# Nearest-neighbour upsampling by two: stores of whole runs against pairs of stores in rows of 512 bytes

## The chip, the cores and the metric

The kernel runs on one core of a Trainium2 chip. The metric is the device time of one execution in microseconds (us); the profiled execution is a separate one, and its span (first to last instruction) is a little shorter than its own time. The engines that do work here are VectorE (DVE) and ScalarE (ACT), which copy, SyncE (SP), which issues transfers, and the 16 DMA engines, which move bytes between DRAM and the on-chip memory (SBUF, 128 partitions).

## The reference

An image batch of 16 x 64 x 64 x 64 float32 is doubled in height and width by repeating each element:

```python
def reference(x, scale_factor):          # scale_factor is 2
    ...
    for i in range(new_h):
        for j in range(new_w):
            src_i = i // scale_factor
            src_j = j // scale_factor
            result[:, :, i, j] = x[:, :, src_i, src_j].copy()
```

So every input element appears four times: twice along its row, and the doubled row (a line of 128 elements, 512 bytes) twice, one below the other. 16.78 MB are read and 67.11 MB written.

## The kernel before

The input's 65,536 rows of 64 elements are spread over the 128 partitions, R = 512 rows to each (`xp`, line 173). An output row of the view `op` (line 174) holds both output lines of one input row, upper then lower, 256 elements or 1 KB, and a partition's 512 output rows are contiguous in DRAM.

The input is loaded whole into `xt`, in three DMAs cut at rows 32 and 288 (lines 192 to 195). `begin_before_barrier` moves these three loads ahead of the program's opening barrier. The output is made in nine chunks of 38 to 63 rows (`rows`, line 181). For each chunk, in the loop from line 204 on, DVE copies the first part of the rows (line 213) and ACT the rest (line 214). `expanded` (line 197) is a view of `xt` in which an element is read twice along its row and each row twice, so the copy writes all four. Then SP issues one store (line 215), whose share in each partition is one contiguous run, both in SBUF and in DRAM: k rows of 1 KB.

The on-chip space is one tile `mem`: 79 rows' worth of free output space, and the input behind it. Even chunks lie at the start of the tile, odd chunks end at the input's first row that hasn't been copied yet, so that output grows into input that is no longer needed. The framework puts in the waits: a copy waits for the load of its rows and for the stores that still read the space it writes, a store waits for the copies of its chunk. All DMAs are issued from SP and go through one queue. `close_early` rearranges the end of the program, so that all but the last store's semaphore are dealt with while that store is under way.

Of the kernel before, what the change touches and what calls it, by code (L numbers as in the profile page):

```python
# [153 lines left out]
@with_exitstack  # L154
def kernel(
    ctx: ExitStack,
    tc: tile.TileContext,
    x: bass.AP,
    scale_factor: int,
    out: bass.AP,  # L160
):
    nc = tc.nc
    nc.at_finalize(begin_before_barrier)
    nc.at_finalize(close_early)
    P = nc.NUM_PARTITIONS
    s = int(scale_factor)
    B, C, H, W = x.shape
    R = B * C * H // P
    fdt = x.dtype

    xp = x.rearrange("b c h w -> (b c h) w").rearrange("(p r) w -> p r w", p=P)
    op = out.rearrange("b c (h hd) w -> (b c h) (hd w)", hd=s).rearrange(
        "(p r) w -> p r w", p=P
    )

    rows = [54, 38, 54, 61, 54, 63, 63, 63, 62]
    GROW = s * s
    FREE = 79
    WF = FREE * GROW * W
    assert sum(rows) == R
    mem_pool = ctx.enter_context(tc.tile_pool(name="mem", bufs=1))
    mem = mem_pool.tile([P, WF + R * W], fdt, name="mem")
    xt = mem[:, WF:].rearrange("p (r w) -> p r w", r=R)

    HEAD = 32
    cuts = [0, HEAD, R // 2 + HEAD, R]
    for lo, hi in zip(cuts, cuts[1:]):
        nc.sync.dma_start(out=xt[:, lo:hi], in_=xp[:, lo:hi])  # L195

    def expanded(r0, r1):
        return (
            xt[:, r0:r1].unsqueeze(2).unsqueeze(4).to_broadcast([P, r1 - r0, s, W, s])
        )  # L200

    r0 = 0
    before = (0, 0)
    for n, k in enumerate(rows):
        size = k * GROW * W
        at = 0 if n % 2 == 0 else WF + r0 * W - size
        assert at >= before[1] or at + size <= before[0]
        before = (at, at + size)
        u = mem[:, at : at + size].rearrange(
            "p (k a w b) -> p k a w b", k=k, a=s, w=W  # L210
        )
        kv = k - 1 if n == 0 else k * 5 // 8 & ~1
        nc.vector.tensor_copy(out=u[:, :kv], in_=expanded(r0, r0 + kv))  # L213
        nc.scalar.copy(out=u[:, kv:], in_=expanded(r0 + kv, r0 + k))  # L214
        nc.sync.dma_start(out=op[:, r0 : r0 + k, :], in_=u)  # L215
        r0 += k


# [33 lines left out]
```

## Time and profile before

| | before |
|---|---|
| runs shown | 197.31 and 197.48 us, median 197.39 |
| profiled execution | 196.92 us, span 195.6 |
| DVE busy | 52.3 us, 9 copies |
| ACT busy | 42.1 us, 9 copies and a table load |
| DMA | 83.89 MB, mean 429 GB/s |
| loads | 1, 8 and 7 MB (1024, 8192 and 7168 KB), landing 4.7, 23.6 and 40.1 us after issue |
| stores | 9 of 4864 to 8064 KB, landing 18.8 to 32.6 us after issue |

The profile counts an engine as busy while it copies. DMA engines are counted apart, as a share of all 16; a transfer's time from issue to landing includes its waiting behind earlier ones in the same queue. Besides the page, the trace keeps a record of every DMA packet with its start, duration and size.

### The profile page before, as it was taken

The page shows a single profiled execution, that of the slowest core. Times are in us where ns is not written, and L with a number is a line of the kernel's source. Part 1 is how long each engine was busy: PE and PEld are TensorE (multiplying, and loading weights), DVE is VectorE, ACT ScalarE, POOL GpSimd, SP SyncE. Part 2 cuts the span into 40 slices and gives each one's busy share as a digit, 9 for nine tenths or more (in the row PEclk, how much of TensorE's full clock was granted, in tenths as well). Part 3 has the DMA queues.
Part 4 walks back from the last instruction along what each step waited for, and adds up shares of the span by engine and source line. Part 5 has one row for each costly group of instructions (what it writes and reads, how often), then busy time and mean ns, then how long its engine had stood idle before and what let it go on. Part 6 is the DMA issues. An engine that isn't in the chain of part 4 may idle for free.

```text
span 195.6 us, 102 instructions
## 1 busy us (share of the span) xinstructions
DVE 52.3 (27%) x9; ACT 42.1 (21%) x10; POOL 0.2 (0%) x4
## 2 busy tenths in 40 slices
DVE  0000099940026091053008204500540073000000
ACT  2000000160029700059500004970000073000000
POOL 0000000000000000000000000000000000000000
DMA  9999989889899989999999899999999999999994
GB/s 429 429 429 429 402 375 563 375 362 543 362 436 390 555 362 418 486 409 409 409 420 532 362 531 433 422 422 422 422 422 422 422 422 422 422 435 545 467 428 208
DMA packets 1728, 83.89 MB, mean 429 GB/s; under 512 B 192, under 2 KB 192, under 8 KB 192
## 3 DMA queue, kind: packets, MB, share of 16 engines
q1 hardware_dynamic: 1728, 83.89, 99.2%
HBM read 16.78 MB, written 67.11 MB: 429 GB/s over the span
## 4 chain that ended last, share of the span: by engine, by line
DMA 65%; ACT 11%; DVE 7%; SPq 0%; issue 0%; DVEq 0%; ACTq 0%
DMA out_dram<-mem 53%; DMA mem<-in_x_dram 12%; ACT mem L214 11%; DVE mem L213 7%; SPq L195 0%; DVEq L213 0%; ACTq L214 0%; SPq L215 0%
## 5 line engine op out<-in xcount | busy, mean ns | idle before, releaser
L213 DVE COPY mem<-mem 128x9728 f32<-128x9728 f32 (+3 forms) x9 | 52.3, 5818 | 110.9 <-DMA out_dram<-mem 86.8
L214 ACT COPY mem<-mem 128x6400 f32<-128x6400 f32 (+5 forms) x9 | 40.8, 4530 | 119.4 <-DMA out_dram<-mem 84.2
L214 ACT ACT_TABLE_LOAD x1 | 1.3, 1283 | 1.7 <-PEq L233 1.7
L233 POOL MEMSET const-bfloat16-1.0<- 128x1 bf16 x1 | 0.1, 102 | 0.0
L233 POOL MEMSET const-uint8-127<- 128x1 uint8 x1 | 0.1, 102 | 0.0
L233 POOL MEMSET const-float32-1.0<- 128x1 f32 x1 | 0.1, 99 | 0.0
L233 POOL MEMSET const-float32-0.0<- 128x1 f32 x1 | 0.1, 98 | 0.2 <-issue 0.2
## 6 DMA issues: line engine op xcount, KB each, us to landing
out_dram<-mem SPq DMA_DIRECT2D x3, 8064.0 KB, 32.4
out_dram<-mem SPq DMA_DIRECT2D x3, 6912.0 KB, 22.9
out_dram<-mem SPq DMA_DIRECT2D x1, 7936.0 KB, 32.3
out_dram<-mem SPq DMA_DIRECT2D x1, 7808.0 KB, 29.3
mem<-in_x_dram SPq DMA_DIRECT2D x1, 7168.0 KB, 40.1
out_dram<-mem SPq DMA_DIRECT2D x1, 4864.0 KB, 26.7
mem<-in_x_dram SPq DMA_DIRECT2D x1, 1024.0 KB, 4.7
mem<-in_x_dram SPq DMA_DIRECT2D x1, 23.6
```

What stands on the lines that cost most here:

```text
L213: nc.vector.tensor_copy(out=u[:, :kv], in_=expanded(r0, r0 + kv))
L214: nc.scalar.copy(out=u[:, kv:], in_=expanded(r0 + kv, r0 + k))
L233: nc = _bacc.Bacc("TRN2", target_bir_lowering=False, num_devices=1)
```

## The change

The copies now double elements along the row only: the wide row (128 elements) is in SBUF once. There are eight chunks of 64 rows, in two buffers of their own, `wide`, beside the whole input. Each chunk is stored by two DMAs from the same SBUF rows: one writes the upper output lines, one the lower. In SBUF a partition's 64 wide rows are contiguous; in DRAM each line of 512 bytes is followed by the 512 bytes of the other line, which the other DMA writes. The first two chunks are copied by ACT alone, chunk 1 first; the others by DVE (40 rows) and ACT (24 rows). The loads are cut at rows 48 and 304.

```diff
-    rows = [54, 38, 54, 61, 54, 63, 63, 63, 62]
-    GROW = s * s
-    FREE = 79
-    WF = FREE * GROW * W
-    assert sum(rows) == R
+    N = 8
+    k = R // N
+    size = k * s * W
     mem_pool = ctx.enter_context(tc.tile_pool(name="mem", bufs=1))
-    mem = mem_pool.tile([P, WF + R * W], fdt, name="mem")
-    xt = mem[:, WF:].rearrange("p (r w) -> p r w", r=R)
-    HEAD = 32
+    xt = mem_pool.tile([P, R, W], fdt, name="x")
+    wide = [mem_pool.tile([P, k, W, s], fdt, name=f"wide{b}") for b in range(2)]
+
+    HEAD = 48
     cuts = [0, HEAD, R // 2 + HEAD, R]
     for lo, hi in zip(cuts, cuts[1:]):
         nc.sync.dma_start(out=xt[:, lo:hi], in_=xp[:, lo:hi])
 
-    def expanded(r0, r1):
-        return (
-            xt[:, r0:r1].unsqueeze(2).unsqueeze(4).to_broadcast([P, r1 - r0, s, W, s])
-        )
-
-    r0 = 0
...
-        kv = k - 1 if n == 0 else k * 5 // 8 & ~1
-        nc.vector.tensor_copy(out=u[:, :kv], in_=expanded(r0, r0 + kv))
-        nc.scalar.copy(out=u[:, kv:], in_=expanded(r0 + kv, r0 + k))
-        nc.sync.dma_start(out=op[:, r0 : r0 + k, :], in_=u)
-        r0 += k
+    def widen(n, kv):
+        u = wide[n % 2]
+        for engine, lo, hi in ((nc.vector.tensor_copy, 0, kv), (nc.scalar.copy, kv, k)):
+            if lo < hi:
+                source = xt[:, n * k + lo : n * k + hi].unsqueeze(3)
+                engine(
+                    out=u[:, lo:hi], in_=source.to_broadcast([P, hi - lo, W, s])
+                )
+
+    def store(n):
+        u = wide[n % 2].rearrange("p k w b -> p k (w b)")
+        lines = op[:, n * k : (n + 1) * k, :].rearrange("p k (a w) -> p k a w", a=s)
+        for a in range(s):
+            nc.sync.dma_start(out=lines[:, :, a], in_=u)
+
+    widen(1, 0)
+    widen(0, 0)
+    store(0)
+    store(1)
+    for n in range(2, N):
+        widen(n, k * 5 // 8)
+        store(n)
```

More of the change, by code (lines that the diff above doesn't have):

```diff
@@ L195 @@
         nc.sync.dma_start(out=xt[:, lo:hi], in_=xp[:, lo:hi])
-    def expanded(r0, r1):
-        return (
-            xt[:, r0:r1].unsqueeze(2).unsqueeze(4).to_broadcast([P, r1 - r0, s, W, s])
-        )
-    r0 = 0
[L203 to L211, printed above, removed]
-        kv = k - 1 if n == 0 else k * 5 // 8 & ~1
-        nc.vector.tensor_copy(out=u[:, :kv], in_=expanded(r0, r0 + kv))
-        nc.scalar.copy(out=u[:, kv:], in_=expanded(r0 + kv, r0 + k))
-        nc.sync.dma_start(out=op[:, r0 : r0 + k, :], in_=u)
-        r0 += k
+    def widen(n, kv):
[18 more added lines that the diff above has]
+        store(n)
 _INS = ['x', 'scale_factor']
```

## The prediction

> **What bounds the kernel now.** I began with the page's DMA rows, because the kernel has nothing but copies and transfers.
>
> ```profile
> DMA  9999989889899989999999899999999999999994
> ...
> q1 hardware_dynamic: 1728, 83.89, 99.2%
> HBM read 16.78 MB, written 67.11 MB: 429 GB/s over the span
> ```
>
> The first line is the busy share of the 16 DMA engines in 40 slices of the 195.6 us span, the second gives the queue's packets, megabytes and share of the engines' time. 1728 packets are 12 transfers (3 loads, 9 stores) of 128 partition rows, 1536 in all, and 16 small packets behind each transfer that raise its semaphore. 99.2% of 195.6 us is 194.0 us of work on each engine. Its sixteenth of the bytes is 5.243 MB, which makes 27.0 GB/s per engine.
>
> Next the rate by stage:
>
> ```profile
> 85.00:120.00 35.00, 9.71 (x3) 10.51 (x3) 0.00 (x0) 1.00 1.00 432
> 120.00:158.00 38.00, 10.47 (x3) 11.09 (x3) 0.00 (x0) 1.00 1.00 435
> ```
>
> The last two columns are the DMA share and GB/s in two stretches of the stores: the engines are full, at 432 to 435 GB/s. Then the chain of work that ended last:
>
> ```profile
> DMA 65%; ACT 11%; DVE 7%; SPq 0%; issue 0%; DVEq 0%; ACTq 0%
> ...
> 0.42 23.59 DMA mem<-in_x_dram
> ...
> 24.11 14.30 DVE mem L213
> ...
> 38.48 18.82 DMA out_dram<-mem
> ```
>
> Read alone it gives ACT and DVE 18% of the span and invites one to shorten copies. It must be laid beside the DMA rows: the chain follows one transfer at a time, and while a copy on it runs another transfer is moving bytes. In the trace's records of single DMA packets 16 are under way (for some ns at a hand-over 17) from the ramp at 1.0 us to 194.8 us, also at 40 us where the last loads hand over to the first store. So the time is the sum of the packets on each engine. A copy counts only if it leaves the queue empty.
>
> **The price of one packet.** In these records a packet lasts its bytes at 27.2 GB/s plus about 8 ns: 38,912 bytes take 1439 ns (1430.6 + 8.4), 55,296 take 2041 (2032.9 + 8.1), 64,512 take 2380 (2371.8 + 8.2), 65,536 take 2418 (2409.4 + 8.6). The next packet on the same engine starts 3 to 4 ns before the end (found by following starts to ends, so an estimate). The net fixed cost is thus 4.2 to 5.1 ns; I take 4.6. The semaphore packets of 4 bytes last 9 ns and overlap by 3 to 6, which nets 3 to 6 ns: the same cost with no data in it.
>
> **Part 1, stores in rows of 512 bytes.** Before, a partition's share of a store is one run of 38 to 63 KB. After, line a of the 64 rows is 64 runs of 512 bytes with 512 bytes skipped between them in DRAM. Bytes stay 67.11 MB. A store DMA has 128 x 64 = 8192 runs, 512 per engine; 16 DMAs make 8192 per engine, where there were 9 x 8 = 72. No packet of such data is in the trace, so its cost is bounded by the rows above: 512 bytes at 27.2 GB/s are 18.8 ns, and the fixed part lies between nothing (runs of one row flow together) and 9 ns (the whole 4-byte packet, with no overlap). I take 4.6 ns, since the net cost is the same from 38,912 to 65,536 bytes and hardly less at 4 bytes, so 512 lies between rows that agree. One run is then 23.4 ns and the stores are 8192 x 23.42 = 191.9 us, where they now are 154.2 us of data plus 72 x 4.6 ns = 154.5 us. **That is +37.4 us**, wholly on the path since nothing but these packets sets it. The ends are +0.1 us and 8192 x 27.8 = 227.9 us, +73.4 us.
>
> The Trainium skill ("DMA: Bandwidth & Descriptors", section "Why small descriptors are slow (HBM only)") puts the cost inside the DMA engine at about 3 cycles for each packet, whatever its size. At the 850 MHz that the page gives that is 3.5 ns, and the sum would by an estimate come to 226 us; the trace's packets, at a net 4.2 to 5.1 ns, show rather more.
>
> **Part 2, the opening.** The loads are cut at rows 48 and 304 instead of 32 and 288. The first two chunks need rows 0 to 127, so both wait for the second load; its 16 further rows (0.52 MB at 435 GB/s) land 1.2 us later, at 24.0 + 1.2 = 25.2 us. Both chunks are then copied by ACT alone, one behind the other, chunk 1 first, each 64 x 128 = 8192 elements. The rows:
>
> ```profile
> L214 ACT COPY mem<-mem 128x6400 f32<-128x6400 f32 x3 | 16.6, 5525 | 24.4 <-DMA out_dram<-mem 24.3
> L214 ACT COPY mem<-mem 128x5632 f32<-128x5632 f32 x2 | 9.8, 4886 | 33.0 <-DMA out_dram<-mem 33.0
> ...
> L214 ACT COPY mem<-mem 128x256 f32<-128x256 f32 x1 | 0.4, 405 | 21.0 <-DMA mem<-in_x_dram 21.0
> ```
>
> The mean ns stands after the busy time. From 5632 to 6400 elements 639 ns are added, 0.832 ns an element; 256 elements leave 192 ns fixed. 8192 elements take 7.0 us, two of them 14.0, so the first store is issued at about 39.3 us where it was 38.48. Its first byte follows some 1.0 us later (as in the first load), at 40.3. The loads' packets end between 39.6 and 40.5 us, depending on the engine. The hole is 0 to 0.8 us; I take 0.3. DVE's 14.3 us at this place goes, which gains nothing, as it was covered by the third load.
>
> **Part 3, half the copying afterwards.** Chunks 2 to 7 give DVE 40 rows (5120 elements) and ACT 24 rows (3072).
>
> ```profile
> L213 DVE COPY mem<-mem 128x9728 f32<-128x9728 f32 x5 | 26.1, 5227 | 59.7 <-DMA out_dram<-mem 59.7
> ...
> L213 DVE COPY mem<-mem 128x13568 f32<-128x13568 f32 x1 | 14.3, 14285 | 24.1 <-DMA mem<-in_x_dram 24.1
> ```
>
> DVE has two speeds here, 0.537 and 1.053 ns an element, so 5120 take 2.75 or 5.4 us; all calls with an even row count are fast, and 40 is even. ACT takes 192 + 3072 x 0.832 ns = 2.75 us. DVE's sum falls from 52.3 to 6 x 2.75 = 16.5 us. I cost that gain at nothing: those 59.7 us of idle time were spent waiting for a store to land.
>
> A new wait comes with the two buffers: chunk n's copies wait until both DMAs of store n-2 have landed. Behind them on SP stand store n's two issues, and nothing else. Meanwhile store n-1 is queued whole, 8.4 MB, 1024 runs per engine, 24.0 us by my price and 19.3 us with no fixed cost. The copy, up to 5.4 us, and about 1 us from issue to first byte fit in. Were the cover gone, 6 x (2.75 + 1.0) = 22 us would be added.
>
> **Part 4, issuing.** SP issues 16 stores instead of 9.
>
> ```profile
> L215 SPq DMA_DIRECT2D out_dram<-mem x9: 332/332/348, 38.5 to 163.2; - x9
> ```
>
> Seven more at 0.33 us are 2.3 us beside 24 us of transfer each time: nothing. All issues of before carry 128 rows, so the trace doesn't show whether one with 8192 runs takes longer.
>
> **Sum.** The profiled execution took 196.92 us (span 195.6 and 1.3 around it). 196.92 + 37.4 + 0.3 = 234.6 us. The median of the runs shown is 0.47 higher at 197.39, so I predict **235 us**.
>
> **Rivals.**
>
> *The runs of a row flow together (not slower).* If the fixed cost is paid once per row and not per 512-byte run, for instance because the skip is only an address step, the stores stay at 154.5 us and the total is 196.9 + 0.1 + 0.3 + 0.5 = 198 us. For it: 8 ns of a packet overlap in part already, and the source is one contiguous run in SBUF. Against: the 4-byte packet nets as much as one of 64 KB, so the cost goes with the packet, not its bytes. It decides below 0.5 ns a run (+4 us). The Trainium skill on the same page (section "Specifications") gives 512 bytes as the smallest transfer that reaches line rate, and by that rule the change is neutral; no transfer in the trace is small enough to test it. Chance 0.09.
>
> *Nothing overlaps with small runs.* If the next run cannot start before the last one's end, the full 8.2 ns count: 8192 x 27.0 = 221.3 us, +66.8, total 264.5 us. For it: the overlap of 3 to 4 ns was seen only where the engine had microseconds to look ahead. Against: the 4-byte packets overlap too. Chance of this or a smaller loss of overlap, 245 to 272 us: 0.20.
>
> *The descriptors aren't made fast enough.* The generator must make 131,072 runs. If all of the 332 ns of an issue went with its 128 rows, 2.6 ns each, they would take 340 us, and the total would be 40 + 340 + 2 = 382 us. It decides from 191.9 us / 131,072 = 1.46 ns a run on, that is, if more than 187 of the 332 ns go with rows. DRAM pages being written in halves would show in the same place. Against: a load and a store issue of 128 rows each, of very different sizes, take 332 to 432 ns, which looks like a cost per instruction. Chance of over 272 us: 0.09.
>
> **Chances and range.** The forecast, 222 to 245 us, has 0.60; with 0.20, 0.09 and 0.09 for the rivals, 0.02 is left for faster, as the data alone need 192.8 us on each engine and no byte is saved. About 2% is what a measurement of this kernel can tell from no change. Slower: 0.60 + 0.20 + 0.09 = 0.89; same 0.09; faster 0.02. The range begins with the smallest net cost of a 4-byte packet, 3 ns: 8192 x 21.8 = 178.8 us, +24.3, 222 us. It ends with 9 ns and no overlap: +73.4 and the larger hole, 272 us. It holds 0.80.
>
> **What would show it.** Right: a store phase at about 350 GB/s (512 B in 23.4 ns on 16 engines) instead of 435, DMA engines still nearly full, mean about 358 GB/s, some 131,000 packets if each run is recorded, first store issued near 39.3 us, DVE and ACT idle for transfers. The flow-together rival would show 432 to 435 GB/s; the generator rival a DMA share well under 1, or SP issues of many microseconds; a lost cover a DMA row with holes between chunks. I'd be wrong if copies of chunks 2 to 7 appeared on a chain with an empty queue beside them.

## The result, and the profile after

The changed kernel takes 276.76 us (median; 276.56 and 276.96) against 197.39 before, a ratio of 1.402 (95% interval 1.396 to 1.408). The prediction was 235 us, in a range of 222 to 272, and the measured time lies above it: the sign and the place were right, the size was about half of what came (38 us forecast, 79 measured).

The page of the changed kernel, its DMA rows (busy share in 40 slices, the moved GB/s under them, then packets, megabytes and share of the 16 engines' time):

```profile
DMA  9999899999999999999999999999999999999998
GB/s 380 457 457 399 371 398 289 251 292 268 307 281 313 294 295 291 289 279 284 285 296 295 277 284 287 303 274 302 284 296 284 292 265 299 288 297 288 290 288 204
...
q1 hardware_dynamic: 131760, 83.89, 110.0%
HBM read 16.78 MB, written 67.11 MB: 304 GB/s over the span
```

131,760 packets are one for each 512-byte run and 688 others (the loads' packets and the small ones that raise semaphores). The engines are as full as before, but from the seventh slice on, where the stores begin, they move about 290 GB/s. A share above 100% means that packets of one engine overlap in the records. The same by stage (DMA share and GB/s are the last two columns):

```profile
100.00:160.00 60.00, 5.66 (x2) 5.51 (x2) 0.00 (x0) 1.00 1.12 288
160.00:220.00 60.00, 8.24 (x3) 8.11 (x3) 0.00 (x0) 1.00 1.12 290
```

In the packet records the stores run from 40.65 to 274.2 us, 233.5 us for 8192 runs on each engine: 28.5 ns a run, 28.4 in the middle. The median packet lasts 27 ns, 18.8 of data and 8.2, as in the long packets of before. But 32% last over 30 ns, and the mean is 32.2. The mean is longer than the 28.4 ns from one run to the next, so packets overlap here too.

The copies and the issues (first the groups: busy, mean ns, idle before; then the stores' issues on SP: shortest, median and longest in ns):

```profile
L198 ACT COPY wide<-x 128x3072 f32<-128x3072 f32 (+1 forms) x8 | 30.4, 3818 | 186.7 <-DMA out_dram<-wide 164.4
L198 DVE COPY wide<-x 128x5120 f32<-128x5120 f32 x6 | 17.0, 2827 | 203.3 <-DMA out_dram<-wide 203.3
```
```profile
L206 SPq DMA_DIRECT2D out_dram<-wide x16: 402/14372/14996, 39.2 to 243.3; - x16
```

DVE's work fell from 52.3 to 17.0 us, and SP, which issues the stores, never waited for it. SP now spends 14.4 us on most issues, and the chain that ended last is full of them:

```profile
SPq 53%; DMA 21%; ACT 5%; DVE 1%; issue 0%; DVEq 0%
```

I read that as a way of seeing the queue, not as a cost. The first issue of 8192 runs took 0.40 us, and the later ones take about as long as one store of 4 MB needs to drain (233.5 / 16 = 14.6): it looks as if an issue is held until there is room behind the transfers ahead of it.

### The profile page after: what moved, and what is told of

Read it like the earlier page. It is cut to its first block, busy times and chain, and to the rows that moved or that the text cites. A ratio compares the mean times of both kernels' runs of the same rounds, so it can differ in the third digit from the quotient of the medians.

```text
span 275.6 us, 101 instructions
## 1 busy us (share of the span) xinstructions
DVE 17.0 (6%) x6; ACT 31.7 (12%) x9; POOL 0.2 (0%) x4
## 2 busy tenths in 40 slices
DMA packets 131760, 83.89 MB, mean 304 GB/s; under 512 B 304, under 2 KB 131376, under 8 KB 131376
## 3 DMA queue, kind: packets, MB, share of 16 engines
q1 hardware_dynamic: 131760, 83.89, 110.0%
## 4 chain that ended last, share of the span: by engine, by line
SPq 53%; DMA 21%; ACT 5%; DVE 1%; issue 0%; DVEq 0%
SPq L206 53%; DMA out_dram<-wide 12%; DMA x<-in_x_dram 9%; ACT wide L198 5%; DVE wide L198 1%; SPq L191 0%; DVEq L198 0%
## 5 line engine op out<-in xcount | busy, mean ns | idle before, releaser
L198 ACT COPY wide<-x 128x3072 f32<-128x3072 f32 (+1 forms) x8 | 30.4, 3818 | 186.7 <-DMA out_dram<-wide 164.4
L198 DVE COPY wide<-x 128x5120 f32<-128x5120 f32 x6 | 17.0, 2827 | 203.3 <-DMA out_dram<-wide 203.3
```

Of the source, the lines that this page charges most:

```text
L198: engine(out=u[:, lo:hi], in_=source.to_broadcast([P, hi - lo, W, s]))
```

## The experiments

The first two kernels were timed four times each, all others once; beside them the kernel before took 197.0 to 197.5 us. "Gapped" means, unless said otherwise, that as many bytes are skipped after each run as it has.

**Which part of the change costs the time?** Two kernels each carry one side of it.

`long_runs` has the changed kernel's input tile, two buffers, load cuts and equal chunks, but both lines made in SBUF:

```diff
-    N = 8
+    N = 16
...
-    wide = [mem_pool.tile([P, k, W, s], fdt, name=f"wide{b}") for b in range(2)]
+    wide = [mem_pool.tile([P, k, s, W, s], fdt, name=f"wide{b}") for b in range(2)]
...
-        for a in range(s):
-            nc.sync.dma_start(out=lines[:, :, a], in_=u)
+        nc.sync.dma_start(out=op[:, n * k : (n + 1) * k, :], in_=wide[n % 2])
```

> Undoes the store form alone: as in the changed kernel two buffers beside the input, the same loads, the first two chunks by ACT alone, equal chunks; but both lines of a row are made in SBUF (16 chunks of 32 rows) and each chunk is one store of 32 KB runs. Copies are doubled again. If the short runs are the whole loss: 197.5 to 199 us. If the buffers, the opening or the waits have a share in it: above 201 us.

It took 198.68 us, 1.007 times before (1.006 to 1.009); its stores move 433 GB/s, those of before 434 in the same window (the first line is `long_runs`, the second before):

```profile
60.00:180.00 120.00, 36.10 (x13) 35.22 (x13) 0.00 (x0) 1.00 1.00 433
60.00:180.00 120.00, 32.39 (x7) 34.08 (x7) 0.00 (x0) 1.00 1.00 434
```

Its first chunk of 32 rows needs only the first load, so its opening is a little earlier than the changed kernel's. The buffers and their waits have no share in the loss worth naming.

`before_split` is the kernel before, with its stores alone changed:

```diff
-        nc.sync.dma_start(out=op[:, r0 : r0 + k, :], in_=u)
+        lines = op[:, r0 : r0 + k, :].rearrange("p k (a w) -> p k a w", a=s)
+        for a in range(s):
+            nc.sync.dma_start(
+                out=lines[:, :, a], in_=u[:, :, a].rearrange("p k w b -> p k (w b)")
+            )
```

> The kernel before with one part of the change alone: each store is two DMAs, of the upper and the lower lines, both from the fully doubled tile; 131,072 runs of 512 bytes, gapped in SBUF and in DRAM. At 28.3 to 29.1 ns a run the stores take 232 to 238 us, the total is 274 to 280 us, about that of the changed kernel, although the copies are those of before. If the SBUF side of the change (one wide row read twice) matters: some other time.

It took 276.38 us, 1.402 times before (1.399 to 1.405): the whole loss, with none of the saved copying.

```profile
60.00:260.00 200.00, 34.99 (x7) 36.75 (x7) 0.00 (x0) 1.00 1.10 289
```

So it is the 512-byte runs. What is left is why one costs 28.4 ns and not 23.4.

**Is it DRAM, the making of runs, or the order of the halves?** Here there are four kernels. `contig_dram` moves the gap from DRAM into SBUF; for that it makes both lines there, in 16 chunks of 32 rows, each stored by one DMA (L is the line, 128 elements):

```diff
-    wide = [mem_pool.tile([P, k, W, s], fdt, name=f"wide{b}") for b in range(2)]
+    wide = [mem_pool.tile([P, k, s, L + 8], fdt, name=f"wide{b}") for b in range(2)]
...
-            nc.sync.dma_start(out=lines[:, :, a], in_=u)
+        nc.sync.dma_start(out=lines, in_=u)
```

> The stores keep runs of 512 bytes (131,072 in all), but the gap is moved: in SBUF each 512-byte line is followed by 32 bytes of padding, in DRAM a partition's share is contiguous. In the changed kernel one engine needed 28.4 ns for a run (233.5 us for 8192), while half of the packets last the 27 ns that were priced. Three theories for the missing 5 ns. T1, the DRAM side: half-lines of 512 bytes with 512 skipped are written badly; then the gap's removal gives 23.4 ns a run and about 235 us. T2, the generator: runs are made at one per 1.77 ns for all engines together, whatever they are; about 277 us. T3, the DMA engine: any 512-byte run costs 28.4 ns; about 277 us. If the writes are joined to long ones again: about 200 us.

264.51 us; 27.3 ns a run, 300 to 301 GB/s:

```profile
120.00:180.00 60.00, 12.01 (x9) 11.82 (x9) 0.00 (x0) 1.00 1.05 300
```

Neither 235 nor 277: at most 1.1 of the missing 5 ns can be laid to the gap in DRAM, and T1 as the main cause falls.

`runs_1k` stores even and odd rows (both lines, 1 KB) in turn:

```diff
-        for a in range(s):
-            nc.sync.dma_start(out=lines[:, :, a], in_=u)
+        for e in range(2):
+            u = wide[n % 2][:, e].rearrange("p k a w b -> p k (a w b)")
+            nc.sync.dma_start(out=lines[:, e], in_=u)
```

> Runs of 1 KB: chunks of 32 rows with both lines in SBUF, even and odd rows stored by two DMAs, so in DRAM 1 KB is written and 1 KB skipped; contiguous in SBUF. 65,536 runs, 4096 per engine. T2 (generator, 1.77 ns a run, 28.4 ns per engine): the engine's own 37.6 + 4.6 = 42.3 ns is longer, so nothing is lost: 173 us of stores, about 216 us. T1 (half-lines in DRAM) and T3 (5 ns more for each run) both: 47.3 ns a run, 194 us of stores, about 236 us.

236.94 us, 47.8 ns a run, 343 GB/s:

```profile
120.00:220.00 100.00, 18.03 (x8) 28.83 (x8) 0.00 (x0) 1.00 1.04 343
```

With half as many runs each costs 5.5 ns more than 42.3, so a generator of one run per 1.77 ns (28.4 ns on each of 16 engines) is not the limit.

`fine_turns` cuts the stores to 8 rows, upper and lower by turns:

```diff
-        for a in range(s):
-            nc.sync.dma_start(out=lines[:, :, a], in_=u)
+        for j in range(0, k, 8):
+            for a in range(s):
+                nc.sync.dma_start(out=lines[:, j : j + 8, a], in_=u[:, j : j + 8])
```

> The changed kernel with its stores cut to 8 rows each, upper and lower lines by turns: the two halves of a 1 KB stretch of DRAM are written some 2 us apart instead of 14. Runs and their number are the same; 128 store DMAs instead of 16. T1: if it is the distance in time of the halves in DRAM, 235 to 260 us. T2 and T3: 277 us, or a few us more for the issues.

280.26 us, 282 GB/s. Having the two halves of a stretch written closer in time gains nothing.

`sbuf_stage` puts these in the place of the stores (stage A, from SBUF to SBUF, over each half of the input tile; stage B, loads in short runs):

```python
for h in range(2):
    pairs = flat[:, h * half : (h + 1) * half].rearrange(
        "p (k a w) -> p k a w", a=s, w=s * W
    )
    for a in range(s):
        nc.sync.dma_start(
            out=pairs[:, :, a], in_=wide[a].rearrange("p k w b -> p k (w b)")
        )
...
for q in range(4):
    ...
    nc.sync.dma_start(out=into, in_=xin[:, q // 2 * k : (q // 2 + 1) * k, q % 2])
```

> A measurement by stages; the output is not the upsampled image. After the loads and the first two wide chunks: stage A, four DMAs of 4 MB from SBUF to SBUF in 512-byte runs (512 skipped in the destination), 2048 runs per engine; stage B, four DMAs of 4 MB that load from DRAM in 512-byte runs (512 skipped in DRAM); stage C, four contiguous stores of 16.8 MB. T1: stage A has no DRAM in it and takes 48 us (23.4 ns a run). T2: 58 us in A and in B, since it is the number of runs that counts. T3: 58 us in both.

Stage A moved 266 GB/s, about 31 ns a run, stage B 287 GB/s, 28.5 ns. A looks like proof that DRAM has no part; `eight_sizes` below shows that A has a price of its own and proves nothing of the kind. B says more: loads in 512-byte runs came to the same rate as the stores, so the loss does not belong to writing alone.

**Is it the size, the side of the gap, or the queue?** Four kernels store straight from the input tile, without copies; here with the run lengths in elements for 2 and 4 KB:

```python
flat = xt.rearrange("p r w -> p (r w)")
span = 2 * R * W
for h, run in enumerate((512, 1024)):
    into = op.rearrange("p r w -> p (r w)")[:, h * span : (h + 1) * span]
    into = into.rearrange("p (k a w) -> p k a w", a=2, w=run)
    for a in range(2):
        nc.sync.dma_start(
            out=into[:, :, a], in_=flat.rearrange("p (k w) -> p k w", w=run)
        )
```

> A measurement; the output is not the upsampled image, nothing is copied. After the loads the input is stored straight from its tile, first 33.5 MB in runs of 2 KB (2 KB skipped in DRAM, two DMAs), then 33.5 MB in runs of 4 KB. So far a 512-byte run cost 27.3 to 30.7 ns on its engine and one of 1 KB 47.8, that is 8.4 to 12 ns beside its bytes at 27.2 GB/s, where packets of 38 KB and more cost 4.6. T5, the hand-over of packets loses its overlap of 4 ns whenever runs are gapped, whatever their size: 2 KB 85 ns a run, 87 us in all; 4 KB 160 ns, 82 us. T6, the loss belongs to small packets only and is gone by 2 KB: 80 ns and 82 us; 155 ns and 79.5 us.

> The same with 256-byte and 8 KB runs. 256 bytes are 9.4 ns of data: with 4.6 ns of fixed cost 8192 runs take 115 us, with 9 ns 151 us, with 12 ns 175 us; far more would mean that something else, per run, begins to bind. 8 KB: 79.6 us by T5 with 10 ns, 78.3 us by T6.

Windows of the first (2 KB, then 4 KB) and of the second (256 bytes, then 8 KB); the last two columns are again DMA share and GB/s:

```profile
50.00:145.00 95.00, 0.00 (x0) 1.00 1.06 310
160.00:220.00 60.00, 0.00 (x0) 1.00 1.02 422
```
```profile
50.00:190.00 140.00, 0.00 (x0) 1.00 0.95 218
205.00:265.00 60.00, 0.00 (x0) 1.00 1.01 421
```

256 bytes cost 18.8 ns, that is 9.4 of data and 9.4; 4 KB cost 155.3, 4.7 beside the data; 8 KB 311, 9.8. So 4 KB came out as T6 has it and 8 KB as T5. At 256 bytes 0.85 runs per ns are made, against 0.56 at 512: a fixed rate of making runs is excluded a second time. 2 KB, at 310 GB/s, is worse than either theory allowed. With the order turned (and on another chip):

> The measurement with 2 KB and 4 KB runs, the order turned: 4 KB first. There 4 KB cost 155 ns a run (4.7 beside the data) and 2 KB 100 to 112 ns where 80 to 85 were expected, with the loss shrinking in time. If it belongs to the 2 KB pattern: 4 KB again 80 us, 2 KB again 102 to 109 us. If it belongs to the first stage after the loads, when the engines start in step: 4 KB now takes 90 us or more, 2 KB 82 to 87 us.

4 KB moved 408 GB/s now, 2 KB 289. That is 160.6 ns for 4 KB, 10.0 beside the data, so these sizes don't decide between T5 and T6. The 2 KB loss belongs to the pattern, not to its place after the loads.

`gap_sides` takes 512-byte runs throughout; parts 2 and 3 read every other line of the tile:

```python
gapped = flat.rearrange("p (k a w) -> p k a w", a=2, w=run)
...
for a in range(2):
    nc.sync.dma_start(out=third[:, a], in_=gapped[:, :, a])
...
for a in range(2):
    nc.sync.dma_start(out=fourth[:, :, a], in_=gapped[:, :, a])
```

> Again stores straight from the input tile, all in 512-byte runs, no copies and no buffers: part 1, 33.5 MB contiguous in SBUF and gapped in DRAM, as in the changed kernel; part 2, 16.8 MB gapped in SBUF and contiguous in DRAM; part 3, 16.8 MB gapped in both. If the cost of a run is the engine's own: 27 to 29 ns in all three, 116, 56 and 58 us. If the gap in DRAM is what makes 28.4 ns of 27.3: parts 1 and 3 at 28.4, part 2 at 27.3. If the copies or the buffers of the changed kernel had a share in it: part 1 at 27 or less.

287, 290 and 281 GB/s in the three parts, 28.5, 28.2 and 29.2 ns a run:

```profile
45.00:155.00 110.00, 0.00 (x0) 1.00 1.15 287
165.00:210.00 45.00, 0.00 (x0) 1.00 1.02 290
225.00:270.00 45.00, 0.00 (x0) 1.00 1.19 281
```

The side of the gap hardly matters, and the changed kernel's rate comes without copies and buffers too.

`two_queues` is the changed kernel with its stores on two queues:

```diff
-        for a in range(s):
-            nc.sync.dma_start(out=lines[:, :, a], in_=u)
+        for a, queue in zip(range(s), (nc.sync, nc.scalar)):
+            queue.dma_start(out=lines[:, :, a], in_=u)
...
-        widen(n, k * 5 // 8)
+        widen(n, k)
```

> The changed kernel with the upper lines' stores issued from SP and the lower lines' from ACT, so that each DMA engine has two queues of runs to take from; chunks 2 to 7 are copied by DVE alone. If the lost overlap is a wait for the next run's descriptor in one queue, the other queue fills it: 23.4 ns a run, about 235 us. If the engine itself can't overlap small packets: 277 us as before. If one generator serves both queues and is the limit: 277 us as well.

279.00 us and 289 GB/s: a second queue fills nothing. The Trainium skill ("DMA: Bandwidth & Descriptors", section "Issuing engines are not separate DMA queues") says that transfers from all issuers run on the same 16 engines and only the issuing time is saved; this run agrees.

**One engine's price, or a price of all together?** A DMA over 8 partitions occupies 8 engines: in the packet records of `eight_engines` 8 to 11 packets are under way at a time, in those of the changed kernel mostly 15 to 22. In `eight_engines` the stores of stage 1 are

```python
for g in range(4):
    short = flat[g:32:4].rearrange("p (k w) -> p k w", w=run)
    for h in range(2):
        into = everything[g:32:4, h * 2 * line : (h + 1) * 2 * line]
        into = into.rearrange("p (k a w) -> p k a w", a=2, w=run)
        for a in range(2):
            nc.sync.dma_start(out=into[:, :, a], in_=short)
```

> A measurement; the output is not the upsampled image. Stage 1 stores 512-byte runs, gapped in DRAM, by DMAs of 8 partitions each (every fourth of the first 32), which occupy 8 DMA engines: 4096 runs per engine. Stage 2 the same in 128 KB rows, 2.1 MB per engine, 77 us at 27.2 GB/s. If the 28.4 ns are the engine's own cost: stage 1 takes 116 us. If they come from what 16 engines share (the supply of runs, the way to DRAM): 23.4 ns or so, 96 us.

The packets last 27 ns (25 to 35), and the rate is steady:

```profile
50.00:130.00 80.00, 0.00 (x0) 1.00 0.57 174
```

174 GB/s on 8 engines are 21.75 GB/s each: 512 bytes in 23.5 ns, the forecast's price to a tenth. So the missing 5 ns are not an engine's own. (Stage 2, with long runs, moved 210 GB/s, some 80 us where 77 were expected.) Two sweeps over the number of engines (the first one's loops; the second takes 12, 14, 16 and 16, every fourth partition):

```python
for stage, engines in enumerate((8, 10, 11)):
    for g in (2 * stage, 2 * stage + 1):
        rows = slice(g, g + 12 * (engines - 1) + 1, 12)
        ...
                nc.sync.dma_start(
                    out=into[:, :, a],
                    in_=flat[rows].rearrange("p (k w) -> p k w", w=run),
                )
```

> A measurement; the output is not the upsampled image. The 512-byte runs, contiguous in SBUF and gapped in DRAM, on 8, then 10, then 11 DMA engines (DMAs of 8, 10 and 11 partitions, every twelfth), 2048 runs per engine and stage. On 8 engines a run took 23.5 ns before, on 16 28.4. S1, a limit on all runs together (16 / 28.4 = 0.564 runs per ns): 11 engines need 0.468, so all three stages keep 23.5 ns and 48 us. S2, pairs of engines i and i+8 share a way: the engines with a partner slow to 28 ns, so 48, then 58 and 58 us. S3, each engine more slows all the others a little: 48, 51 and 52 us.

> A measurement; the output is not the upsampled image. As the engine sweep, with 12, 14, 16 and 16 engines (DMAs of as many partitions, every fourth from 32 on, one partition to an engine), 1024 runs of 512 bytes per engine and stage. 8, 10 and 11 engines kept 23.5 ns a run. S1, a limit on all runs together at 0.56 to 0.59 per ns: 12 engines (0.51) keep 23.5 ns, 14 (0.595) just touch it, 16 need 27.3 to 28.4 ns: 24, 24 to 25 and 28 to 29 us. S4, it is not the number of engines but the form of the transfer over 128 partitions (8 partitions to an engine, whose rows lie 512 KB apart in DRAM): 23.5 ns and 24 us in every stage.

The stages with 8, 10 and 11 engines, then in the second kernel 12, 14 and twice 16:

```profile
45.00:85.00 40.00, 0.00 (x0) 1.00 0.57 174
92.00:132.00 40.00, 0.00 (x0) 1.00 0.72 217
140.00:180.00 40.00, 0.00 (x0) 1.00 0.79 239
```
```profile
46.00:62.00 16.00, 0.00 (x0) 1.00 0.86 261
66.00:74.00 8.00, 0.00 (x0) 1.00 0.99 300
80.00:110.00 30.00, 0.00 (x0) 1.00 1.00 287
110.00:145.00 35.00, 0.00 (x0) 1.00 1.01 287
```

Up to 12 engines the rate is 21.7 to 21.75 GB/s for each; 14 give 300 instead of 304.5; 16 give 287 instead of 348, less than 14. Pairs of engines (S2) would have shown at 10 and 11, a loss with each engine (S3) from 8 to 12. The form over 128 partitions (S4) falls too, since here an engine has one partition. What binds is something that all 512-byte runs share, near 290 to 300 GB/s; it is no constant limit, as 16 engines get less than 14.

The same DMAs on 8 engines with `run` at 64, 256 and 512 elements, after a stage between two SBUF tiles:

> A measurement; the output is not the upsampled image. 8 engines again. Stage A: 512-byte runs from SBUF to SBUF, 512 per engine; then stores to DRAM in runs of 256 bytes (4096 per engine), 1 KB (1024) and 2 KB (512). If 8 engines disturb each other nowhere, each run costs its bytes at 27.2 GB/s and 4.6 ns: 12.0 us in A (30.7 ns a run on 16 engines would be 15.7), then 57, 43 and 41 us (on 16 engines 77, 49 and 51 to 60). If the loss on 16 engines was DRAM's alone: A would have shown none on 16 engines, and takes 15.7 us here too. If the 2 KB loss belongs to its addresses and not to the number of engines: 51 to 60 us for 2 KB.

Its windows (SBUF to SBUF, 256 bytes, 1 KB, 2 KB):

```profile
45.00:57.00 12.00, 0.00 (x0) 1.00 0.53 131
62.00:112.00 50.00, 0.00 (x0) 1.00 0.64 145
120.00:155.00 35.00, 0.00 (x0) 1.00 0.54 193
162.00:195.00 33.00, 0.00 (x0) 1.00 0.53 205
```

On 8 engines 256 bytes, 1 KB and 2 KB cost 14.1, 42.4 and 79.9 ns: bytes at 27.2 GB/s and 4.7 ns, each time. The 2 KB loss is gone as well. Only stage A (SBUF to SBUF) is slow here too, at 31 ns a run; at that price 16 engines ask for no more than 266 GB/s, which is below the shared limit, so A can't show it.

And on 16 engines, with `rows = slice(first, first + 61, 4)`:

> A measurement; the output is not the upsampled image. DMAs of 16 partitions on 16 engines, one partition to each, in runs of 256 bytes (2048 per engine), 1 KB (512), 2 KB (256) and 4 KB (128). S1: the losses of the 128-partition transfers come back: 18.8, 47.8, 100 to 118 and 155 to 160 ns a run, so 38.6, 24.5, 26 to 30 and 20 us. S4: 14.1, 42.4, 79.9 and 155.3 ns as on 8 engines, so 28.9, 21.7, 20.5 and 19.9 us.

Its windows (256 bytes, 1 KB, 2 KB, 4 KB; one partition to an engine):

```profile
45.00:78.00 33.00, 0.00 (x0) 1.00 0.96 217
83.00:105.00 22.00, 0.00 (x0) 1.00 1.09 303
110.00:130.00 20.00, 0.00 (x0) 1.00 1.06 347
136.00:150.00 14.00, 0.00 (x0) 1.00 1.02 422
```

The prices of 8 engines (bytes at 27.2 GB/s and 4.7 ns) would give 290, 386, 410 and 422 GB/s. So a loss came back except at 4 KB, which speaks for S1, but not in the sizes that S1 was given: 256 bytes cost 18.9 ns (18.8 over 128 partitions), 1 KB more (54.1 ns against 47.8) and 2 KB less (94.4 against 105.7 and 113.4). The form of the transfer may have a share at 1 and 2 KB; these are single runs on different chips.

## Why the prediction was too low

**What bounds the kernel** held in its first half: the DMA engines have no hole, and as before the chain misleads (53% of SP now, 18% of copies then). That the time is the sum of the packets, each at a price of its own engine, did not hold.

**The step that failed is Part 1's price of a run**, 23.4 ns taken where 28.4 were measured. It is a mis-sized term: the stores took 233.5 us, not 191.9, and these 41.6 us are nearly the whole miss (276.96 - 234.6 = 42.4). The price was right for an engine: 23.5 ns as long as 8 to 12 of them work, and on 8 engines one fixed cost of 4.7 ns at four sizes. What was wrong is the silent step behind it, that 16 engines with small packets go on as independently as 16 with large ones. The rows of before could not show it: there a store's packets, 38 KB or more, follow each other on an engine every 1.4 us or later, here every 28 ns. The upper end failed for the same reason: 27.8 ns was the dearest that one engine's own records allowed, and the loss appears only when more engines work at once.

**The rivals.** "Flow together" is refuted (a store phase of 288 to 290 GB/s, where it asked for 432 to 435). The Trainium skill's 512 bytes for line rate ("DMA: Bandwidth & Descriptors", section "Specifications") don't hold here: 290 against 434 GB/s for long runs. "Nothing overlaps" gave the closest time (264.5 us) by luck, since its mechanism is wrong: on 8 engines the overlap is there, with 27 ns packets every 23.5 ns, and in the changed kernel too, with packets of 32.2 ns on average every 28.4. "Not made fast enough" named a limit shared by all engines, which was the right kind, but as a rate of runs it is refuted by 0.85 per ns at 256 bytes; and its sign, long issues on SP, appeared without it. That sign was badly chosen.

**The other parts** held. The first store was issued at 39.25 us (forecast 39.3), its first packet came at 40.65 as the last loads ended, so the hole of 0.3 us is nearly nothing. (The loads' last packets before end between 40.04 and 40.61 us in the records, not between 39.6 and 40.5 as the prediction has it; nothing hangs on that.) The copies took 2.75 us on ACT (forecast 2.75) and 2.83 on DVE (2.75), always behind a full queue, so the new wait between chunk n and store n-2 cost nothing.

**What stays open** is what the 16 engines share. Over 128 partitions the times for 256 and 512 bytes (1.17 and 1.77 ns per run in total) fit 0.58 ns a run plus the bytes at 433 GB/s, and that line gives 347 GB/s for 1 KB (343 measured), 408 for 4 KB (408 and 422) and 420 for 8 KB (421). That describes the loss; it does not name its place, and it isn't a law: 14 engines move more 512-byte runs (300 GB/s) than the line's 290, and with one partition to an engine 1 KB reached 303 only. 2 KB falls below the line (385 against 289 and 310, and 347 with one partition to an engine), and only with 16 engines; its cause wasn't found. One rival was not tried: in all these kernels the partitions' shares of the output lie 512 KB, or a multiple of it, apart in DRAM (those of the input 128 KB). Whether the shared limit or the 2 KB loss hangs on these addresses is open, and so is whether loads on 8 engines are free of the loss.

## What to carry to other kernels

A packet's price read from a few large packets was a lower bound: with all 16 engines on runs of 256 or 512 bytes the fixed cost here doubled, from 4.7 to about 9.5 ns per run and engine. With the DMA engines full, the work saved on the copy engines was worth nothing (`before_split`, which saves none, takes the same 276 us), and the runs cut to 512 bytes were paid in full, while runs of 4 or 8 KB lost 3 to 6% of the rate. Doubling the lines in SBUF, by copies hidden behind the transfers, was cheaper than leaving it to the stores (`long_runs`, 198.68 us). A long issue on the chain of waits may be only a full queue: look at the shortest issue of the same size.

## What the runs showed that was not expected

16 engines move 512-byte runs more slowly (287 GB/s) than 14 do (300). Runs of 2 KB with 2 KB skipped, at 289 to 310 GB/s over 128 partitions, are slower than 1 KB runs with 1 KB skipped (343); with one partition to an engine it is the other way round (347 and 303). 256-byte stores show no further step down: on 8 engines they have the same fixed cost of 4.7 ns as 512 bytes (145 and 174 GB/s), on 16 about the same 9.5 (218 and 287). A copy from SBUF to SBUF in 512-byte runs costs 31 ns a run on 8 and on 16 engines alike.
